# A decoder trunk on one core: a fourth weight block summed by an accumulating transfer, and table transfers moved ahead of the first MLP

## The chip, the cores and the metric

The kernel runs on 1 core of a Trainium2 chip. The metric is the device time of one execution in microseconds (us), as the median of several runs.

Engines are named as in the profile: PE (TensorE, matrix products), PEld (its weight loads), DVE (VectorE), ACT (ScalarE), POOL (GpSimd), SP (SyncE). SP and POOL each issue transfers (DMAs) in the order of their own queue. A transfer issued by POOL can add what it brings to what lies at its destination; this is called an accumulating transfer here.

## The reference, cut to what matters

A two-layer decoder trunk on 512 tokens of width 1024, all in float32. Layer 0 is attention and an MLP, layer 1 a gated short convolution and an MLP:

```python
def conv_ffn(h, norm_g, w_up, conv_w, w_down):
    xn = rms_norm(h, norm_g)
    u = causal_dwconv(xn @ w_up, conv_w)          # w_up: 1024 x 5632, conv over 3 tokens
    g, val = u[..., :D_FF], u[..., D_FF:]         # D_FF = 2816
    return (jax.nn.silu(g) * val) @ w_down

h = x
for layer in range(DEPTH):                        # DEPTH = 2
    i = layer // 2
    if layer % 2 == 0:
        h = h + attention_mixer(h, ...)
    else:
        h = h + short_conv_mixer(h, ...)
    h = h + conv_ffn(h, ffn_norm[layer], ffn_w_up[layer], ffn_conv[layer], ffn_w_down[layer])
```

## The kernel before

Float32 operands are split into a high and a low half (`whi` on ACT, `wlo` on DVE), and each product is three matmuls (high by high, high by low, low by high). The activations lie with features on the partitions and 512 tokens in the free dimension.

**The up-projection with seven products.** Most of the up-projection is not done as a plain product. The weight of one group (256 gate columns and the 256 value columns that belong to them) is cut in two halves of the depth (512 rows each) and two halves of the columns (gate, value), which gives four blocks of 512 x 256; the tokens are cut in two halves as well. A Strassen-like scheme (`Sevens`) then makes the result with seven products of half size, called p1, p7, p3, p6, p2, q5, q4. Their weights are sums of blocks with one, two, three or four members. In the code a block is `block_of(g, kh, half)`: `kh` the half of the depth, `half` 0 for gate and 1 for value.

- X is the block (0, 0), used for p1; afterwards POOL adds the block (0, 1) to it in place (L1105), and the sum serves q5.
- Y serves p7; it is a sum of two blocks.
- "three" serves p6, a sum of three blocks; "four" serves q4, the sum of all four.
- W is the block (1, 0), for p2; Z the block (1, 1), for p3.

X and Y have two buffers each. W, Z, three and four come into the ring `raw` (three buffers of 128 x 1056 numbers).

`Sevens.slot(g, s)` issues one product in slot s = 0 to 6 of group g (p3 of the group before stands in slot 2), and around it the loads, splits and evacuations that come due. The first MLP makes its groups 0 and 1 by plain products (`PLAIN`) and groups 2 to 10 in this way; the second MLP makes all eleven so. Small pieces of other work ("chores", with costs and a credit) are strewn between the slots.

**The tables.** The sums for Y, three and (in the first MLP only) four are not made on DVE. POOL makes them ahead of time in DRAM: `table_steps(layer)` is a generator of which each step issues one DRAM-to-DRAM transfer, in turn a plain copy (L117) and an accumulating one (L114). Table 7 is block (1, 1) plus block (0, 1); table 6 is a copy of table 7 plus (0, 0); table 4 is a copy of table 6 plus (1, 0). The groups are taken in three chunks (`CHUNKS`), the 512 rows in two parts. So the first MLP has 3 x 2 x 6 = 36 steps, the second 3 x 2 x 4 = 24. Each step but the first of a table part waits for the step before it, since it reads or adds to what that one wrote. `pin` keeps instructions in the order of the program on their queue.

Where the steps are issued:

- the 36 steps of the first MLP between the units of attention, two in each unit;
- 8 steps of the second MLP (`FAR`) after attention, ahead of the output projection's end;
- 9 (`BETWEEN`) at the end of `mlp(0, ...)`, after its last product; since POOL's queue runs ahead of PE, these start when POOL's last transfer for the down-projection is out;
- the last 7 in the convolution layer (`sum_far(99)`).

**In the second MLP** there is no table 4: once p6 has taken its halves from "three", an accumulating transfer adds the block (1, 0) to it in place (slot 2), and q4 takes its halves from the same buffer. In the last group DVE adds W to it instead. The lines of slot 2 that choose:

```python
if self.fours:
    self.load_one(g, "four", self.table("4", g))
else:
    c["four"] = c["three" if self.table else "Y"]
    if self.scaled and soon:
        self.add_block(g, "four", 1, 0)
    else:
        dve.tensor_tensor(c["four"], c["four"], c["W"], op=ALU.add)
```

`fours` is true for the first MLP, `scaled` for the second, `soon` as long as a group follows. The convolution layer uses `Sevens` with no tables.

**The down-projections** (L1673) use seven products too. Their weight blocks come by SP (L285, L291) and by accumulating transfers of POOL (L289) into buffers whose names end in "chain"; for q5 some are loaded as "other" and added on DVE (L286). Around the same time POOL adds halves of the activations (`head_blocks`, `hs_b_blocks`, L1070). Weights of plain products are loaded by SP at L309 into raw and split at L315 (ACT) and L316 (DVE).

Of the kernel before, what the change touches and what calls it, by code (L numbers as in the profile page):

```python
# [22 lines left out]
ALU = mybir.AluOpType  # L23
# [24 lines left out]
FILL1, FILL2, BEFORE = 1.5, 3.3, 2.0  # L48
UNITS = (0, 1), (2,), (3,)
PLAIN = 2, 0  # L50
FAR, BETWEEN = 8, 9
CHUNKS = ((2, 3), (5, 3), (8, 3)), ((0, 3), (3, 4), (7, 4))
EARLY, LATER = 4.0, 5.0
SHARE = 0.58
# [3 lines left out]
def trunk(  # L58
# [9 lines left out]
    class InOrder:  # L68
        def __init__(self, engine):
            self.engine = engine  # L70
# [6 lines left out]
    act, dve, pe, pool = InOrder(nc.scalar), InOrder(nc.vector), nc.tensor, nc.gpsimd  # L77
# [19 lines left out]
    tables = {}  # L97

    def table_steps(layer):

        w = ffn_w_up[layer]
        for n in "76" if layer else "764":
            for g, m in CHUNKS[layer]:
                tables[layer, n, g] = far.tile([512, m * 256 + 16], F32, tag=f"t{layer}{n}{g}", name=f"t{layer}{n}{g}")
        def block(kh, half, g, m):
            return w[kh * 512:(kh + 1) * 512, half * DFF + g * 256:half * DFF + (g + m) * 256]
        for g, m in CHUNKS[layer]:
            for rows in (slice(0, 256), slice(256, 512)):
                for step in range(4 if layer else 6):
                    n = "764"[step // 2]  # L110
                    to = tables[layer, n, g][rows, 0:m * 256]
                    if step % 2:
                        src = block(*((0, 1), (0, 0), (1, 0))[step // 2], g, m)
                        pin(nc.gpsimd.dma_start(to, src[rows, :], accum_op=ALU.add))  # L114
                    else:
                        src = block(1, 1, g, m) if step == 0 else tables[layer, "76"[step // 2 - 1], g][:, 0:m * 256]
                        pin(nc.gpsimd.dma_start(to, src[rows, :]))  # L117
                    yield

    def table_of(layer, n, group):  # L120
        g, m = next(c for c in CHUNKS[layer] if c[0] <= group < c[0] + c[1])
        return tables[layer, n, g][:, (group - g) * 256:(group - g + 1) * 256].rearrange("(k p) c -> p k c", p=P)
# [128 lines left out]
    def fill(us):  # L251
        quota[0] += us
        while quota[0] > 0 and fillers:
            before = clock[0]
            if next(fillers[0], None) is None:
                fillers.pop(0)
            quota[0] -= clock[0] - before

    def run(gen):
        for _ in gen:  # L260
            pass
# [582 lines left out]
    def output_begin():  # L844
        last_w.append([weights(), weights(AHEAD - 1)])
        yield from output_part(range(4), range(2), "b")
        last_w.append([weights(AHEAD - 1), weights(0)])
        yield from output_part(range(4), (2,), "b")
# [116 lines left out]
            fillers.append(values(g + 1))  # L965
    units = [(p, u) for p in range(8) for u in range(len(UNITS))]
    waiting = {}
    sums_far = table_steps(0)
    next(sums_far)
    fill(PRE)  # L970
    for g in range(len(units) + 2):
        for _ in range(2):
            next(sums_far, None)
        if g < len(units):
            waiting[g] = logits(*units[g])
            fill(FILL1)
        if g == len(units):
            fillers.append(output_begin())
            fill(BEFORE)
        if g >= 2 and units[g - 2][1] == len(UNITS) - 1:  # L980
            p = units[g - 2][0]
            weigh(p)
            if p == 3:
                fillers.append(output(0, residual))
        if 1 <= g <= len(units):
            for b, w in waiting.pop(g - 1):
                turn(units[g - 1][0], b, w)
                fill(FILL2 / len(UNITS[units[g - 1][1]]))
    fill(1e9)

    run(sums_far)
    sums_far = table_steps(1)

    def sum_far(n):
        for _ in range(n):
            next(sums_far, None)

    sum_far(FAR)

    def residual_out(o, acc, nxt):  # L1000
        dve.tensor_tensor(h[:, o, :], acc, h[:, o, :], op=ALU.add)
# [81 lines left out]
    class Sevens:  # L1083

        def __init__(self, name, mp, groups, block_of):
            self.name, self.mp, self.groups, self.block_of = name, mp, groups, block_of
            self.forms = {n: [mp.tile([P, 4, HT], F32R, tag=f"{n}_{i}", name=f"{n}_{i}{name}") for i in ("hi", "lo")] for n in FORMS}
            self.st, self.wides, self.table, self.fours, self.scaled = {}, {}, None, False, False

        def load_pair(self, g):  # L1090
            s = self.st[g] = {}
# [66 lines left out]
        def slot(self, g, s):  # L1158

            on, was, soon = (i in self.groups for i in (g, g - 1, g + 1))  # L1160
            if self.chores:
                self.work_off(self.rate(g, s))
            form, n, fresh = (("p1", "A", True), ("p7", "T", True), ("p3", "R", False), ("p6", "R", False), ("p2", "A", False),
                              ("q5", "R", False), ("q4", "T", False))[s]
            if s == 2:
                if was:
                    self.product(g - 1, form, n, fresh)
            elif on:
                self.product(g, form, n, fresh)
            st, p, c = self.st, g - 1, self.st.get(g)  # L1170
            if s == 0:
                if was:
                    if "p3" not in st[p]:
                        self.weights_of(p, "p3", "Z")
                    self.join(p, "yg", st[p]["T"], st[p]["Xs"])
                if on:
                    self.load_one(g, "W", self.block_of(g, 1, 0))
                if soon:
                    self.load_pair(g + 1)
            elif s == 1:  # L1180
                first = not was
                if on and first and not self.ahead and "p6" not in c:
                    self.weights_of(g, "p6", "three" if self.table else "Y")
                if on:
                    act.activation(self.bank_of(g, "R"), c["A"], AF.Copy, scale=-1.0)
                if on and not first:
                    self.weights_of(g, "p6", "three" if self.table else "Y")
                if soon and not self.table:
                    self.add_block(g + 1, "Y", 1, 1)
            elif s == 2:  # L1190
                if on:
                    self.kept(g, "P7s", c["T"])
                    if "p2" not in c:
                        self.weights_of(g, "p2", "W")
                    if self.fours:
                        self.load_one(g, "four", self.table("4", g))
                    else:
                        c["four"] = c["three" if self.table else "Y"]
                        if self.scaled and soon:
                            self.add_block(g, "four", 1, 0)  # L1200
                        else:
                            dve.tensor_tensor(c["four"], c["four"], c["W"], op=ALU.add)
            elif s == 3:
                if was:
                    self.early(p, st[p]["R"])
                if on:
                    self.weights_of(g, "q5", "X")
            elif s == 4:
                if on:
                    self.kept(g, "Xs", c["R"])  # L1210
                    self.weights_of(g, "q4", "four")
            if was and s != 2:
                self.tail(p, s)
            if s == 5:
                if on:
                    self.load_one(g, "Z", self.block_of(g, 1, 1))
                    self.open_wides(g)
                    self.left(g, c["A"])
                if soon:
                    self.weights_of(g + 1, "p1", "X")  # L1220
                elif on and self.ahead:
                    self.weights_of(g, "p3", "Z")
            elif s == 6:
                if on:
                    self.join(g, "yv", c["R"], c["P7s"])
                if soon:
                    self.first_sums(g + 1)
# [17 lines left out]
    def up_begin(layer, norm, mp, place):  # L1245
# [4 lines left out]
        w_up, base = ffn_w_up[layer], PLAIN[layer]  # L1250
# [5 lines left out]
        up = Sevens(layer, mp, range(base, HF), block_of)  # L1256
        up.norm, up.chores = norm, []
        up.table = lambda n, g: table_of(layer, n, g)
        up.fours, up.scaled = layer == 0, not base
        up.rate = lambda g, s: 1.4 if g == base else 0.3 if layer else 0.5  # L1260

        def wides_of(g):
# [249 lines left out]
    def mlp(layer, norm, mp, begun_up=None):  # L1512
# [21 lines left out]
        def block(kh, ch, k0, fresh):  # L1534
            return (ffn_w_down[layer], kh * HF + k0, ch * 512), fresh
# [165 lines left out]
                    finish(b)  # L1701
        if after_:
            after_.finish()
            sum_far(BETWEEN)
        return after_

    with tc.tile_pool(name="mlp0", bufs=1, reuse_waits="tile") as mp:
# [6 lines left out]
    with tc.tile_pool(name="mlp1", bufs=1, reuse_waits="tile") as mp:  # L1714
        norm = Norm("n3", 8)
        blocks, up = up_begin(1, norm, mp, rp)
# [77 lines left out]
```

## Time and profile before

| | us |
|---|---|
| runs | 1122.01, 1123.62, 1126.45 (median 1123.62) |
| profiled execution | 1121.57 |
| its span in the profile | 1119.8 |
| PE busy, DVE busy, ACT busy, POOL busy | 1109.3, 958.8, 680.4, 174.3 |

How to read it: the profile is one execution; times inside it count from the start of its span. PE is busy for nearly the whole span, but a matmul is counted as busy from its start to its modelled end, and matmuls overlap, so short holes do not show in the busy time; the number of matmuls in a stretch shows them. The stages by time: attention with its output projection and then the plain groups of the first MLP to 320, its seven-product groups to about 496, its down-projection to about 611, the convolution layer to about 783, the second MLP to the end. The granted PE clock is 1.00 throughout.

### The profile page before, as it was taken

To read this page: it belongs to the slowest core of one execution; us is meant where nothing else is said; L and a number is where in the kernel's file an instruction comes from. 1 tells how busy PE (TensorE), PEld (TensorE's weight loads), DVE (VectorE), ACT (ScalarE), POOL (GpSimd) and SP (SyncE) were. 2 spreads that over 40 slices of the span, in tenths; PEclk is the share of its full clock that TensorE was granted. 3 is DMA by queue.
4 is the path that set the end of the run, shared out by engine and by line. 5 is a ranking of instruction groups with operands and counts; after the bars stand their busy time and mean duration, and the time that the engine had idled before them with its cause. 6 is when DMAs were issued, how large, how long until landed. Compare 5 with 4: busy or idle time off the path is not lost.

```text
span 1119.8 us, 19731 instructions
## 1 busy us (share of the span) xinstructions
PE 1109.3 (99%) x7803; PEld 1011.9 (90%) x7803; DVE 958.8 (86%) x1482; ACT 680.4 (61%) x1006; POOL 174.3 (16%) x203
## 2 busy tenths in 40 slices
PE   9999999999999999999999999999999999999998
PEld 7888787878899999999999889988999999998886
DVE  6798988987899787888979899767899999999886
ACT  7466676655466667676547355445666656667553
POOL 4011111111111110014401101110112221014300
PEclk9999999999999999999999999999999999999999
DMA  6668777677888787699997955697879877899951
GB/s 195 178 175 199 177 186 196 164 197 196 245 206 199 189 212 192 195 297 198 224 260 195 238 143 141 130 275 178 207 179 218 204 189 189 217 262 205 230 154 57
DMA packets 180012, 220.90 MB, mean 197 GB/s; under 512 B 7788, under 2 KB 143516, under 8 KB 179920
## 3 DMA queue, kind: packets, MB, share of 16 engines
q0 software_dynamic: 48384, 97.43, 43.9%
q1 hardware_dynamic: 131376, 122.14, 34.7%
q8 instruction: 61, 1.00, 0.4%
q14 instruction: 31, 0.25, 0.1%
q10 hardware_dynamic: 160, 0.07, 0.0%
HBM read 214.64 MB, written 53.48 MB: 239 GB/s over the span
## 4 chain that ended last, share of the span: by engine, by line
PE 82%; DVE 7%; DMA 5%; issue 3%; ACT 2%; SPq 0%; ACTq 0%; DVEq 0%; POOLq 0%
PE psb L1078 28%; PE psa L1078 11%; PE psb L1673 10%; PE psa L1673 7%; PE psb L336 4%; PE psb L338 4%; PE psb L337 4%; PE psb L710 2%; PE psa L807 2%; DVE wlo L316 1%; DMA Xc<-in_conv_w_in 1%; DMA raw<-in_conv_w_in 1%; DMA raw<-in_conv_w_out 1%; PE psc L782 1%; PE psa L338 1%
## 5 line engine op out<-in xcount | busy, mean ns | idle before, releaser
L1078 PE MATMUL psb<-p_lo,whi_p 128*128 128x256 f32 x480 | 135.1, 282 | 0.0
L315 ACT ACTIVATE whi<-raw 128x1024 fp32r<-128x1024 f32 (+2 forms) x81 | 83.3, 1029 | 85.3 <-PE psb L337 27.9
L1078 PE MATMUL psb<-p_hi,wlo_p 128*128 128x256 f32 x480 | 135.0, 282 | 0.0
L1078 PE MATMUL psb<-p_hi,whi_p 128*128 128x256 f32 x480 | 134.8, 281 | 0.0
L316 DVE TENSOR_TENSOR wlo<-raw,whi 128x1024 fp32r<-128x1024 f32 (+2 forms) x81 | 95.8, 1183 | 28.0 <-ACT whi L315 27.6
L1078 PEld LDWEIGHTS psb<-p_hi,whi_p 128*128 128x128 f32 x480 | 90.9, 189 | 0.0
L1078 PE MATMUL psb<-q_hi,whi_q 128*128 128x256 f32 x320 | 89.9, 281 | 0.5 <-ACT whi_q L74 0.5
L1078 PEld LDWEIGHTS psb<-p_lo,whi_p 128*128 128x128 f32 x480 | 90.4, 188 | 0.0
L1078 PEld LDWEIGHTS psb<-p_hi,wlo_p 128*128 128x128 f32 x480 | 90.2, 188 | 0.1
L1078 PE MATMUL psa<-p_hi,wlo_p 128*128 128x256 f32 x320 | 90.1, 282 | 0.0
L1078 PE MATMUL psa<-p_lo,whi_p 128*128 128x256 f32 x320 | 90.1, 281 | 0.0
L1078 PE MATMUL psb<-q_lo,whi_q 128*128 128x256 f32 x320 | 90.0, 281 | 0.0
L1078 PE MATMUL psb<-q_hi,wlo_q 128*128 128x256 f32 x320 | 89.9, 281 | 0.0
L1078 PE MATMUL psa<-p_hi,whi_p 128*128 128x256 f32 x320 | 89.8, 281 | 0.0
L336 PE MATMUL psb<-hs_a,whi 128*128 128x512 f32 x192 | 79.3, 413 | 0.0
L338 PE MATMUL psb<-hs_a,wlo 128*128 128x512 f32 x192 | 76.3, 398 | 0.0
L1673 PE MATMUL psb<-act,whi 128*128 128x256 f32 x352 | 63.1, 282 | 0.5 <-DVE act L1031 0.4
L1078 PEld LDWEIGHTS psb<-q_hi,whi_q 128*128 128x128 f32 x320 | 60.6, 189 | 0.8 <-ACT whi_q L74 0.8
L1078 PEld LDWEIGHTS psa<-p_hi,whi_p 128*128 128x128 f32 x320 | 60.6, 190 | 0.1
L1078 PEld LDWEIGHTS psa<-p_lo,whi_p 128*128 128x128 f32 x320 | 60.2, 188 | 0.1
L1078 PEld LDWEIGHTS psb<-q_lo,whi_q 128*128 128x128 f32 x320 | 60.2, 188 | 0.0
L1078 PEld LDWEIGHTS psa<-p_hi,wlo_p 128*128 128x128 f32 x320 | 60.2, 188 | 0.0
(553 smaller groups left out, 3593.6 us busy)
## 6 DMA issues: line engine op xcount, KB each, us to landing
t<-in_ffn_w_up POOLq DMA_DIRECT2D x30, 768.0 KB, 7.8
raw<-in_attn_w_in SPq DMA_DIRECT2D x24, 512.0 KB, 5.4
t<-in_ffn_w_up POOLq DMA_DIRECT2D x12, 1024.0 KB, 10.9
t<-t POOLq DMA_DIRECT2D x14, 768.0 KB, 4.7
X<-in_ffn_w_up SPq DMA_DIRECT2D x20, 512.0 KB, 5.0
Y<-t SPq DMA_DIRECT2D x20, 512.0 KB, 6.7
three<-t SPq DMA_DIRECT2D x20, 512.0 KB, 4.8
W<-in_ffn_w_up SPq DMA_DIRECT2D x20, 512.0 KB, 4.0
```

The source lines that it names most:

```text
L315: return (act.activation(hi[:, at_], raw[:, at_], AF.Copy), dve.tensor_tensor(lo[:, at_], raw[:, at_], f32(hi[:, at_]), op=ALU.subtract))
L316: dve.tensor_tensor(lo[:, at_], raw[:, at_], f32(hi[:, at_]), op=ALU.subtract))
L336: made = [pe.matmul(acc, w[0], rhs[0], start=first, stop=False), pe.matmul(acc, w[0], rhs[1], start=False, stop=False), pe.matmul(acc, w[1 ...
L337: pe.matmul(acc, w[0], rhs[1], start=False, stop=False),
L338: pe.matmul(acc, w[1], rhs[0], start=False, stop=last)]
L710: pe.matmul(ss[e][:, c:c + wide], ql[rows, b * P:n], kl[rows, 0:wide], start=first and b == bs[0], stop=last and b == bs[-1])
L782: pe.transpose(t[:, k * P:(k + 1) * P], w[:, e, k * P:(k + 1) * P], ident)
L807: pe.matmul(out_, w, t[:, first:first + step * (NB - k - 1) + 1:step, :], start=k == 0 and i == 0, stop=k == NB - 1 and i == 1)
L1078: pe.matmul(to, w[a][:, k, c], x[b][:, k, :], start=fresh and i + k + t == 0, stop=i == 1 and k == 3 and t == 2, skip_group_check=not fresh)
L1673: pe.matmul(to, l, r, start=begin and o + t == 0, stop=end and t == 2 and o == (0 if layer else 1), skip_group_check=not fresh)
```

## The change

The first MLP has no table 4 any more: `table_steps` makes tables 7 and 6 for both layers, so the first MLP has 24 steps instead of 36. In slot 2 the branch `fours` is gone, and the accumulating transfer into "three" is used wherever there are tables and a group follows, in the first MLP too: in its groups 2 to 9 POOL adds the block (1, 0) to "three" where SP loaded "four", and in group 10 DVE adds W to it.

The steps of both layers become one generator, issued from the units of attention: one step ahead, and then two in each unit until `FAR` = 41 are out, that is the 24 of the first MLP and 17 of the second. The 8 steps after attention and the 9 at the end of the first MLP are gone from there; the last 7 stay in the convolution layer.

```diff
-FAR, BETWEEN = 8, 9
+FAR = 41
...
-        for n in "76" if layer else "764":
+        for n in "76":
...
-                for step in range(4 if layer else 6):
-                    n = "764"[step // 2]
+                for step in range(4):
+                    n = "76"[step // 2]
...
-    sums_far = table_steps(0)
-    next(sums_far)
+
+    def both_layers():
+        for layer in range(2):
+            yield from table_steps(layer)
+
+    sums_far = both_layers()
+
+    def sum_far(n):
+        for _ in range(n):
+            next(sums_far, None)
+
+    sum_far(1)
     fill(PRE)
     for g in range(len(units) + 2):
-        for _ in range(2):
-            next(sums_far, None)
+        sum_far(max(0, min(2, FAR - 1 - 2 * g)))
...
-    run(sums_far)
-    sums_far = table_steps(1)
-
-    def sum_far(n):
-        for _ in range(n):
-            next(sums_far, None)
-
-    sum_far(FAR)
...
-                    if self.fours:
-                        self.load_one(g, "four", self.table("4", g))
+                    c["four"] = c["three" if self.table else "Y"]
+                    if self.table and soon:
+                        self.add_block(g, "four", 1, 0)
                     else:
-                        c["four"] = c["three" if self.table else "Y"]
-                        if self.scaled and soon:
-                            self.add_block(g, "four", 1, 0)
-                        else:
-                            dve.tensor_tensor(c["four"], c["four"], c["W"], op=ALU.add)
+                        dve.tensor_tensor(c["four"], c["four"], c["W"], op=ALU.add)
...
-        up.fours, up.scaled = layer == 0, not base
+        up.scaled = not base
...
             after_.finish()
-            sum_far(BETWEEN)
```

More of the change, by code (lines that the diff above doesn't have):

```diff
@@ L108, in table_steps @@
             for rows in (slice(0, 256), slice(256, 512)):
-                for step in range(4 if layer else 6):
-                    n = "764"[step // 2]
+                for step in range(4):
+                    n = "76"[step // 2]
                     to = tables[layer, n, g][rows, 0:m * 256]
                     if step % 2:
-                        src = block(*((0, 1), (0, 0), (1, 0))[step // 2], g, m)
+                        src = block(*((0, 1), (0, 0))[step // 2], g, m)
                         pin(nc.gpsimd.dma_start(to, src[rows, :], accum_op=ALU.add))
                     else:
-                        src = block(1, 1, g, m) if step == 0 else tables[layer, "76"[step // 2 - 1], g][:, 0:m * 256]
+                        src = block(1, 1, g, m) if step == 0 else tables[layer, "7", g][:, 0:m * 256]
                         pin(nc.gpsimd.dma_start(to, src[rows, :]))
@@ L1087, in __init__ @@
             self.forms = {n: [mp.tile([P, 4, HT], F32R, tag=f"{n}_{i}", name=f"{n}_{i}{name}") for i in ("hi", "lo")] for n in FORMS}
-            self.st, self.wides, self.table, self.fours, self.scaled = {}, {}, None, False, False
+            self.st, self.wides, self.table, self.scaled = {}, {}, None, False
         def load_pair(self, g):
```

## The prediction

> **What bounds the kernel now.** I read the page first (busy time, then the chain that ended last), then the stretches by time with their counts of matmuls, then the instructions of POOL in order, and last the DVE, ACT and landing rows around the places where TensorE (PE) was late.
>
> ```profile
> span 1119.8 us, 19731 instructions
> PE 1109.3 (99%) x7803; PEld 1011.9 (90%) x7803; DVE 958.8 (86%) x1482; ACT 680.4 (61%) x1006; POOL 174.3 (16%) x203
> PE 82%; DVE 7%; DMA 5%; issue 3%; ACT 2%; SPq 0%; ACTq 0%; DVEq 0%; POOLq 0%
> ```
>
> PE is the bound. Its busy share hides short gaps, though, so I count matmuls. The columns below are the stretch, its length, and busy time with count for PE, PEld, DVE, ACT, POOL, then granted clock, DMA share and GB/s.
>
> ```profile
> 340.00:480.00 140.00, 140.00 (x1186) 140.00 (x1185) 115.92 (x144) 93.54 (x121) 15.25 (x13) 1.00 0.73 194
> 520.00:560.00 40.00, 40.00 (x340) 40.00 (x340) 36.73 (x53) 23.51 (x32) 17.05 (x17) 1.00 1.03 213
> 560.00:600.00 40.00, 38.56 (x321) 37.95 (x320) 32.43 (x43) 21.07 (x31) 2.92 (x4) 1.00 0.94 255
> 600.00:610.00 10.00, 9.95 (x84) 9.75 (x83) 8.85 (x13) 7.82 (x12) 0.88 (x1) 1.00 0.61 145
> 660.00:670.00 10.00, 9.39 (x77) 8.99 (x76) 9.10 (x8) 6.91 (x9) 2.58 (x2) 1.00 0.88 174
> 820.00:1000.00 180.00, 180.00 (x1524) 180.00 (x1523) 169.91 (x217) 114.24 (x140) 31.83 (x26) 1.00 0.85 208
> 1060.00:1100.00 40.00, 40.00 (x174) 32.08 (x173) 33.50 (x43) 23.38 (x32) 2.42 (x2) 1.00 0.52 131
> ```
>
> The up-projections of both MLPs (340 to 480, 820 to 1000) run at 118 ns for each 128x256 matmul (140/1186, 180/1524), without a hole. So nothing that is taken from DMA or DVE there can shorten them; a change can only open a hole. Holes are at 560 to 610, in the down-projection of the first MLP: 321 matmuls where the 40 us before hold 340, and 84 where 85 fit. 20 missing matmuls of 0.118 us make 2.4 us. At 660 to 670 (start of the convolution layer) 8 are missing, 0.9 us. The same down-projection stage of the second MLP (1060 to 1100, 128x512 matmuls of 230 ns) has no hole.
>
> What is late at 560 to 600 is weights. In the chain that ended last, and in the landing times of the stretch 555 to 612 (first three issue rows) against 1060 to 1116 in the second MLP (last two):
>
> ```profile
> 564.02 8.58 DMA raw<-in_ffn_w_down
> 622.97 13.81 DMA raw<-in_conv_w_in
> ...
> t<-in_ffn_w_up POOLq DMA_DIRECT2D x5, 1024.0 KB, 10.7
> raw<-in_ffn_w_down SPq DMA_DIRECT2D x2, 512.0 KB, 8.6
> other<-in_ffn_w_down SPq DMA_DIRECT2D x2, 512.0 KB, 5.4
> ...
> raw<-in_ffn_w_down SPq DMA_DIRECT2D x2, 512.0 KB, 5.2
> other<-in_ffn_w_down SPq DMA_DIRECT2D x2, 512.0 KB, 3.4
> ```
>
> The same loads land in 8.6 and 5.4 us in the first MLP and in 5.2 and 3.4 us in the second. The first has the table transfers of the second MLP beside them (t, 1024 KB each), and these are what the change moves away. POOL's rows in order of time (start, duration):
>
> ```profile
> 40.20 0.59 POOL L117 DMA_DIRECT2D t<-in_ffn_w_up  x1
> 258.98 0.88 POOL L117 DMA_DIRECT2D t<-in_ffn_w_up  x1
> 283.41 0.91 POOL L117 DMA_DIRECT2D t<-in_ffn_w_up  x1
> 304.33 0.89 POOL L114 DMA_DIRECT2D t<-in_ffn_w_up  x1 [3.99 <-DMA t<-t]
> 319.48 1.34 POOL L1105 DMA_DIRECT2D X<-in_ffn_w_up  x1 [14.26 <-DVE wlo_p L1029]
> 557.68 1.09 POOL L117 DMA_DIRECT2D t<-in_ffn_w_up  x1
> 620.87 0.88 POOL L117 DMA_DIRECT2D t<-in_ffn_w_up  x1
> ```
>
> The nine steps written behind the first MLP start at 557.68, as soon as POOL's last sum for the down-projection is issued, and go on to 620.87.
>
> **The change part by part.**
>
> *Nine table steps leave 557 to 621.* Gain between 0 (the loads are late for another reason) and 2.4 us (all 20 matmuls). I take 2.4: the second MLP, with the same loads and no table beside them, is whole. Behind it the 13.81 us load of convolution weights, which ran beside the last tables, held ACT 1.78 us and through it DVE 1.25 us:
>
> ```profile
> 636.88 1.06 ACT L315 ACTIVATE whi<-raw 128x1024 fp32r<-128x1024 f32 x1 [1.78 <-DMA raw<-in_conv_w_in]
> 637.98 1.23 DVE L316 TENSOR_TENSOR wlo<-raw,whi 128x1024 fp32r<-128x1024 f32 x1 [1.25 <-ACT whi L315]
> ```
>
> DVE then works without pause until the hole at 660 to 670. Between 0 and 0.9 us comes back; I take 0.6, since DVE's backlog there is mostly its own work (9.10 of 10 us). Late next is that DVE backlog.
>
> *The table steps before the first MLP.* They are a chain on POOL, each waiting for the transfer before it, so their time is transfer time. Now 36 steps of the first MLP run from 40.20 to 258.98 (six units of six, 36.5 us each); a unit of four with 768 KB steps takes 283.41 - 258.98 = 24.4 us. After: six units of 24.4 for the first MLP, two more for the second, then two with 1024 KB (4/3 of it, 32.6): 40.2 + 195 + 65 = 300.5, where the 17th step of the second MLP is issued, to land some 10.7 later, at 311. Now the last one before the first MLP is issued at 304.33. The stream is as long as before and carries the same bytes (32 of 768 KB and 9 of 1024 against 44 of 768). POOL has nothing else until X at 319.48. I cost this at nothing. The cover is that no engine but POOL waits for table transfers in attention; if it failed, the 17th step would have to slip 19 us before X is issued late. The seven steps left stay in the convolution layer.
>
> *Eight accumulating transfers in the first MLP.* For each of the groups 2 to 9, SP's load of four (512 KB) and its place in the ring raw go; POOL issues a transfer that adds a fourth block into three, once both halves of p6 have been taken from it. That is a new wait, on wlo_p<-three; behind it on POOL stands only the next block sum or X, over 10 us later. The second MLP does exactly this now. Rows for one group of the first MLP, its first group, and landing times (min/median/max) of three in 820 to 1000 and of X in 335 to 480:
>
> ```profile
> 401.61 1.22 DVE L1029 TENSOR_TENSOR wlo_p<-three,whi_p 128x1024 fp32r<-128x1024 f32 x1
> 408.72 1.05 ACT L1027 ACTIVATE whi_q<-four 128x1024 fp32r<-128x1024 f32 x1
> 410.07 1.22 DVE L1029 TENSOR_TENSOR wlo_q<-four,whi_q 128x1024 fp32r<-128x1024 f32 x1
> 411.01 5.70 PE psb L1078 x48
> ...
> 321.56 1.23 DVE L1029 TENSOR_TENSOR wlo_p<-three,whi_p 128x1024 fp32r<-128x1024 f32 x1
> 329.26 1.05 ACT L1027 ACTIVATE whi_q<-four 128x1024 fp32r<-128x1024 f32 x1
> 331.51 5.67 PE psb L1078 x48
> ...
> L1105 POOL DMA_DIRECT2D three<-in_ffn_w_up x8: 1283/1283/1296, 830.7 to 968.7; - x8
> DMA to landing us min/median/max: 5.1/5.7/6.4
> ...
> DMA to landing us min/median/max: 4.8/6.3/8.9
> ...
> PE psb L1078 <- ACT whi_q L74: 0.5, 1, 0.5
> ```
>
> The add can go at 402.83, say 403.0; at 5.7 us it lands at 408.7, when ACT takes four today. The 48 matmuls from 411.01 are q5 and q4, so q4 begins at 413.86 and wants wlo_q at 414.1 (its third product). Today wlo_q ends at 411.29, 2.8 us before that, so the add may land as late as 411.5: 8.5 us after its issue. With the second MLP's 5.1 to 6.4 nothing stalls; with the slowest X (8.9) 0.4 us in a group. I take 0 for the seven steady groups, nearest to the row of the same transfer. In the first group the add goes at 323.0 and lands between 328.7 (5.7 us) and 331.9 (8.9 us). ACT takes four at 329.26 today, so it would be held for up to 2.6 us; q4 begins at 331.51 + 2.84 = 334.35 and is still served, but the split for the next group moves close to its use. The second MLP's first group lost 0.5 us of PE to this very transfer (last row, from PE's waits in 780 to 1000). Cost between 0 and 1.5 (a landing of 10.8, below); I take 0.5.
>
> Issue took 1.28 us and landing at most 6.4 in the second MLP, beside a DVE busy 169.91 of 180 us. [...]
>
> *Group 10 adds on DVE* (no next group), where four was a load. In the second MLP:
>
> ```profile
> L1202 DVE TENSOR_TENSOR three<-three,W x1: 1215/1215/1215, 988.9 to 988.9; 128x1024 f32<-128x1024 f32 x1
> ```
>
> 1.2 us on DVE, covered by its idle time (115.92 of 140 us busy in 340 to 480), 1.2 on the path if that is gone; the second MLP shows no hole after it. I take 0. SP loses nine issues; it is not on the chain.
>
> Sum: -2.4 - 0.6 + 0.5 = -2.5 us. Against the profiled execution (1121.57 us, span 1119.8) that is 1119.1; the median of the runs shown, 1123.62, lies 2.05 above it, so 1121.1, rounded 1121.0.
>
> **The rivals.**
>
> *Order, not traffic.* The loads at 560 to 600 are late because SP issues them late (buffers), and stay late without the tables. For it: waits of SP for DVE's splits are its longest. Against: the landing itself, from issue, is 8.6 against 5.2. Gain 0, cost 0.5: 1124.1.
>
> *Adds that land late (the other side).* Place: ACT's split of four at q4, in groups 2 to 9. It opens a hole once a landing exceeds 8.5 us, and decides from 9.6 on ((5.6 + 3.3) / 8 = 1.1 us in each group). Accumulating transfers in a crowded stretch do take that long:
>
> ```profile
> X_chain<-in_ffn_w_down POOLq DMA_DIRECT2D x4, 512.0 KB, 10.8
> ```
>
> At 10.8: 2.3 x 8 = 18.4 us, less 3.3 of gain: 1138.7. Against: the stretch in question moves 194 GB/s, less than the second MLP's 208, where 6.4 was the worst. I leave it 0.08, since the first MLP orders its ACT work otherwise. [...]
>
> *More than the holes counted.* All 3.3 us come back, the first group costs nothing, and attention gains some 2.4 us from tables that load it differently: 1117.9. Against: in 40 to 320 PE waits for no transfer.
>
> *A table stream that ends too late.* 7% longer units put the 17th step at 319.5 and X behind it. X lands at 327 now and its next use by PE (q5) is at 331.51, so a slip of 26 us (10%) costs about 4 us: 1123.62 - 3.3 + 4 = 1124.3.
>
> **How the numbers follow.** Forecast 0.60 (1121.0), order 0.18, late adds 0.08, more 0.10, late stream 0.04. A measurement of this kernel tells about 0.5%, 5.6 us, from no change (its runs spread 1122.01 to 1126.45). Below 1118.0 lies only "more": faster 0.10. Above 1129.2 late adds, and 0.02 of a worse late stream: slower 0.10. The rest, same 0.80. The range goes from all gains with a run at the low end of the spread (1123.62 - 4.7 - 1.6 = 1117.3, so 1117) to no gain with 1.5 us of cost and 0.9 of spread (1126). The likeliest case alone spans 1119 to 1123.
>
> **What the changed profile would show.** Right: no t row on POOL between 311 and 700; raw<-in_ffn_w_down landing in about 5 us and 340 matmuls in the 40 us that answer to 560 to 600; about 85 in the 10 us at the start of the convolution groups; three<-in_ffn_w_up 18 times instead of 10, landing below 8.5 us, no four<-t, and 8.47 matmuls a microsecond kept through the first up-projection; the last early t on POOL near 300. Wrong: PE waiting for whi_q or wlo_q in the first MLP, t rows still running beside X at 319, or holes at 560 to 600 that stay with no table beside them.

## The result and the profile after

| | before | after |
|---|---|---|
| median of 14 runs each, us | 1122.65 (1120.97 to 1126.45) | 1120.09 (1119.51 to 1122.06) |
| ratio, 95% interval | | 0.9978 (0.9969 to 0.9987) |
| profiled execution and its span, us | 1121.57, 1119.8 | 1119.51, 1117.7 |

The kernel became 2.6 us faster by the medians and 2.1 us by the profiled executions, about 0.2%: a small gain, but the interval leaves out 1. From the page of after: the span, the busy times, and the shares of the chain that ended last.

```profile
span 1117.7 us, 19713 instructions
PE 1110.0 (99%) x7803; PEld 1013.5 (91%) x7803; DVE 960.4 (86%) x1483; ACT 681.6 (61%) x1006; POOL 174.7 (16%) x199
PE 91%; DVE 4%; DMA 2%; ACT 1%; issue 1%; SPq 1%; DVEq 0%; ACTq 0%
```

PE's busy time hardly differs (1109.3 before, 1110.0 now); what differs is the chain: 5% of the span hung on DMA before, 2% now. The same stretches by time as in the prediction follow (stretch, length, busy time and count of PE, PEld, DVE, ACT, POOL, clock, DMA share, GB/s). The start of the convolution groups lies 2 us earlier now, so it is read at 658 to 668.

```profile
340.00:480.00 140.00, 140.00 (x1186) 140.00 (x1185) 115.55 (x143) 94.02 (x121) 24.41 (x20) 1.00 0.81 193
560.00:600.00 40.00, 39.97 (x338) 39.77 (x337) 34.40 (x46) 22.64 (x33) 1.30 (x1) 1.00 0.59 157
598.00:608.00 10.00, 9.92 (x84) 9.71 (x84) 8.85 (x13) 7.55 (x11) 0.00 (x0) 1.00 0.03 5
658.00:668.00 10.00, 10.00 (x85) 9.84 (x84) 8.43 (x8) 6.59 (x10) 2.29 (x2) 1.00 0.94 196
820.00:1000.00 180.00, 180.00 (x1518) 180.00 (x1517) 169.39 (x215) 113.38 (x139) 31.22 (x26) 1.00 0.85 205
```

321 matmuls at 560 to 600 have become 338 (340 would fill it), and the 10 us at the start of the convolution layer hold 85 instead of 77. The first up-projection still holds 1186 in 140 us: the eight accumulating transfers opened no hole. The issues of 555 to 612, with the median time to the landing (from the issue until the data are there):

```profile
raw<-in_conv_w_in SPq DMA_DIRECT2D x4, 512.0 KB, 3.8
raw<-in_ffn_w_down SPq DMA_DIRECT2D x2, 512.0 KB, 6.8
other<-in_ffn_w_down SPq DMA_DIRECT2D x2, 512.0 KB, 3.8
```

The down-projection's weights land in 6.8 and 3.8 us, where they took 8.6 and 5.4. These medians stand on few loads: `raw` x2 has only one landing on record in either run, and not that of the same load. Load by load, the second of `raw` took 8.2 us in the first experiment below, with the table steps beside it, and 6.8 in after; the third took 8.6 in before and 4.7 in the second experiment, without them. Of the two of `other`, one went from 7.7 to 4.4, and the other stayed (3.2 and 3.3). POOL's rows in order of time (start, duration), and the rows of the tile `three` in 320 to 480 (durations in ns, first and last start, landing times, who waited):

```profile
40.42 0.59 POOL L117 DMA_DIRECT2D t<-in_ffn_w_up  x1
280.86 0.90 POOL L117 DMA_DIRECT2D t<-in_ffn_w_up  x1
319.70 1.36 POOL L1105 DMA_DIRECT2D X<-in_ffn_w_up  x1 [37.94 <-DVE wlo_p L1029]
323.31 1.29 POOL L1105 DMA_DIRECT2D three<-in_ffn_w_up  x1 [2.24 <-DMA Z<-in_ffn_w_up]
...
L1105 POOL DMA_DIRECT2D three<-in_ffn_w_up x8: 1273/1288/1303, 323.3 to 463.4; - x8
...
DMA to landing us min/median/max: 3.7/5.9/7.2
```

The last early table step leaves at 280.86, 39 us ahead of X, and the longest landing is 7.2 us, where the prediction gave 8.5 as the slack.

To place the gain, the i-th matmul of before was set against the i-th of after (after minus before, by their starts in the two profiled executions): +0.23 us up to 570, -1.73 at 600, -2.67 at 670, -3.03 at 720, then -2.1 at the end. So 2.0 us come from the down-projection, 0.9 from the start of the convolution layer and 0.4 from small holes up to 720. Of the 0.9 us given back, 0.2 lie between 783 and 820, where PE waits 0.2 us for a value of DVE at 785, and 0.7 in the second up-projection, where this execution's matmuls came a little slower (1518 in 180 us against 1524), on which more below.

### The profile page after: what moved, and what is told of

Same layout as the page of the kernel before. It is cut to its first block, busy times and chain, and to the rows that moved or that the text cites. A ratio compares the mean times of both kernels' runs of the same rounds, so it can differ in the third digit from the quotient of the medians.

```text
span 1117.7 us, 19713 instructions
## 1 busy us (share of the span) xinstructions
PE 1110.0 (99%) x7803; PEld 1013.5 (91%) x7803; DVE 960.4 (86%) x1483; ACT 681.6 (61%) x1006; POOL 174.7 (16%) x199
## 4 chain that ended last, share of the span: by engine, by line
PE 91%; DVE 4%; DMA 2%; ACT 1%; issue 1%; SPq 1%; DVEq 0%; ACTq 0%
PE psb L1078 30%; PE psa L1078 12%; PE psb L1670 11%; PE psa L1670 8%; PE psb L336 5%; PE psb L338 5%; PE psb L337 5%; PE psb L710 2%; PE psa L807 2%; PE psa L338 1%; DMA raw<-in_conv_w_out 1%; PE psa L337 1%; PE psa L336 1%; PE psc L782 1%; PE psb L592 1%
```

## The experiments

Two theories were set against each other. **Traffic**: the nine table transfers, running beside the last weight loads of the first down-projection, made those loads late; moving them is the gain. **Adds**: the gain comes from table 4 and the loads of `four` being dropped (10 MB of 221 MB less to move), and the place of the steps matters little. In each session the kernel before ran beside the edited ones on the same chip (its medians were 1123.5 to 1124.7, against the 1122.65 above), and a ratio is always to these runs; times of different sessions compare less well.

**Nine steps put back behind the first MLP**, all else as after:

```diff
-FAR = 41
+FAR, BETWEEN = 32, 9
...
             after_.finish()
+            sum_far(BETWEEN)
```

> The changed kernel with nine of its seventeen early steps of the second MLP's tables put back at the end of the first MLP (32 steps in attention, 9 behind the down-projection); the accumulating transfers and the missing table 4 stay. Traffic theory (the nine transfers beside the last weight loads make the holes): the holes at 560 to 610 and 660 to 670 come back, some 2.0 and 0.9 us, and the time is that of the kernel before, 1122.6 us (ratio 1.000). Adds theory (fewer bytes and no loads of four make the gain): no holes, 1120.1 (ratio 0.998).

Measured: 1122.04 us, ratio to before 0.9993 (0.9972 to 1.0014). Its stretches, and its issues in 555 to 612:

```profile
560.00:600.00 40.00, 38.10 (x317) 37.50 (x317) 31.96 (x42) 20.98 (x31) 2.92 (x4) 1.00 0.92 246
658.00:668.00 10.00, 9.68 (x79) 9.27 (x78) 9.26 (x10) 5.64 (x8) 2.58 (x2) 1.00 0.72 134
```

```profile
t<-in_ffn_w_up POOLq DMA_DIRECT2D x5, 1024.0 KB, 10.9
raw<-in_conv_w_in SPq DMA_DIRECT2D x3, 512.0 KB, 5.8
raw<-in_ffn_w_down SPq DMA_DIRECT2D x2, 512.0 KB, 8.2
other<-in_ffn_w_down SPq DMA_DIRECT2D x2, 512.0 KB, 5.6
```

Both holes are back, with landings as late as before, although table 4 stays dropped. By the matmul's index this execution loses 0.5 us on before between 560 and 600, where after gains 2.0, and gains 0.3 at the start of the convolution layer, where after gains 0.9; the profiled execution (1122.23) is no shorter than before's (1121.57). The times alone don't decide: the interval of the ratio holds both forecasts, 1.000 and 0.998. The traces do, and Traffic holds for both holes. It is not shown for the 0.4 us up to 720: the small hole there closes in this run too (0.7 us between 700 and 720), with the steps back.

**The move alone**: the kernel before, with table 4 and the loads of `four` kept; the nine steps are strewn over the slots of the first MLP's groups:

```diff
-FAR, BETWEEN = 8, 9
+FAR = 8
...
+            if layer == 0 and i % 7 == 3:
+                sum_far(1)
...
-            sum_far(BETWEEN)
```

> The kernel before, with table 4 and SP's loads of four kept, and only the nine steps moved: one in slot 3 of each of the groups 2 to 10 of the first MLP, where POOL is idle for most of 20 us. Traffic theory: holes at 560 to 610 and 660 to 670 go, 1120.0 us (ratio 0.998), as with the whole change. Adds theory: nothing gained, 1122.6 (ratio 1.000).

Measured: 1120.75 us, ratio 0.9968 (0.9952 to 0.9983).

```profile
340.00:480.00 140.00, 140.00 (x1186) 140.00 (x1185) 116.00 (x143) 94.21 (x122) 20.87 (x20) 1.00 0.93 247
560.00:600.00 40.00, 39.97 (x338) 39.77 (x338) 34.52 (x47) 22.65 (x33) 1.28 (x1) 1.00 0.61 160
658.00:668.00 10.00, 10.00 (x85) 9.84 (x85) 9.13 (x9) 6.61 (x9) 2.60 (x2) 1.00 0.84 156
```

The holes are gone without a single byte dropped: Adds falls as the source of the gain. The up-projection carries 247 GB/s (193 in after) and keeps its 1186 matmuls, so that stage had room for the nine steps. One hole of about a microsecond appeared at 508 (PE waited 0.7 us for `wlo` of a weight); its cause is open.

**Five of the nine back** (`FAR, BETWEEN = 36, 5`, else as the first experiment):

> As e1_nine_back, but only five steps behind the down-projection (36 in attention). They run from 557 to about 604. Traffic theory, hole by hole: the holes at 560 to 600 come back in full (2.0 us), the one at 660 to 670 stays away, since no table is beside the convolution's first weights; 1122.1 us less what the second hole is worth, so about 1121.9. If the hole at 660 to 670 came from DVE's own backlog and not from the late load, it comes back too: 1122.6.

Measured: 1122.83 us, ratio 0.9985 (0.9970 to 1.0000).

```profile
560.00:600.00 40.00, 39.05 (x328) 38.64 (x327) 33.13 (x45) 22.31 (x32) 4.28 (x5) 1.00 0.95 255
658.00:668.00 10.00, 10.00 (x85) 9.84 (x84) 9.24 (x9) 6.25 (x8) 2.60 (x2) 1.00 0.69 111
```

The five steps run from 559 to about 600. The hole beside them is back in part (328 matmuls, between 317 and 338; 1.2 us late by the matmul's index, less than the 2.0 expected), and the one at 660, which they no longer reach, stays closed. PE's waits in 560 to 605, first with nine steps back, then with five:

```profile
572.30 0.39 PE L1670 MATMUL psa<-act,whi 128*128 128x256 f32 x1 [0.82 <-DVE act L1031]
576.07 0.39 PE L1670 MATMUL psa<-act,whi 128*128 128x256 f32 x1 [0.68 <-DVE act L1031]
592.36 0.39 PE L1670 MATMUL psb<-act,whi 128*128 128x256 f32 x1 [0.40 <-DVE act L1031]
...
573.65 0.39 PE L1670 MATMUL psa<-act,whi 128*128 128x256 f32 x1 [0.92 <-DVE act L1031]
```

Only the first of the three waits is left, although the same five steps run beside this stretch in both. DVE splits the third load of `raw` at the same time (574.19 and 574.20), but PE comes 1.3 us later here, mostly since its matmuls ran slower before (1181 in 340 to 480 against 1186), so it has less to wait for. So where the steps are decides whether there is a hole, but not alone how deep it is. The hole at 660 has a second possible cause that no run separates: with nine steps ahead of it, POOL's own sum into `Yc` for the convolution layer is issued at 621.44 in before instead of 592.98 in after and 596.10 here, and is then in flight beside the 13.81 us load as well. The times of the first and this run overlap: for the split between the holes only the traces speak.

**No accumulating transfer in the first MLP**: DVE adds W instead, table 4 stays dropped.

```diff
-                    if self.table and soon:
+                    if self.scaled and soon:
```

> The changed kernel with the fourth block added by DVE in groups 2 to 9 of the first MLP as well (1.2 us each), so no accumulating transfer into three there. If the transfer costs nothing where it is and DVE has 1.2 us to spare in each group of 20 (it is busy 83% there): same time, 1120.1 within 0.5 us, and no hole from 340 to 480. If DVE's order is the limit: up to 8 x 1.2 = 9.6 us more, 1129.7.

Measured: 1121.22 us, ratio 0.9969 (0.9954 to 0.9985). DVE is 9 us busier in 340 to 480 and PE has no hole there:

```profile
340.00:480.00 140.00, 140.00 (x1181) 140.00 (x1181) 124.58 (x152) 93.58 (x122) 15.37 (x13) 1.00 0.65 168
```

The ratio is that of the second experiment (0.9968), so the accumulating transfer itself carries nothing of the gain that can be seen, and the sum could be made on DVE. The time is 1.1 us above the 1120.1 that was expected within 0.5: by the matmul's index the profiled execution gains the holes (1.3 of the 2.0 us between 570 and 600, 0.9 at the start of the convolution layer), and loses 1.0 to a slower pace of matmuls up to 570 and 1.3 between 900 and 960, where PE waits 0.7 us for `wlo_q` of DVE. That wait stands in some runs and not in others (0.5 us with the nine steps back, none in before and after); why is open.

**All seventeen steps before the first MLP, with table 4 kept** (the kernel before with `FAR = 17` and no steps behind the first MLP):

> The kernel before with table 4 kept, and all seventeen steps of the second MLP behind the 36 of the first, ahead of the first MLP: what moving alone gives if table 4 stays. By the length of the stream (36.5 us for a unit of six, 24.4 and 32.6 for the units of the second MLP) the seventeenth step is issued at 259 + 49 + 65 = 373 instead of 300, so the transfer into X of group 2, due at 319.5, is issued some 54 us late on POOL, and q5 of the first group waits for it. PE's slack there is about 4 us: about 50 us more, 1172. If POOL's order did not matter, 1120.

Measured: 1171.55 us (two runs, 1168.07 and 1175.03), ratio 1.0419 (1.0375 to 1.0463). POOL's rows, PE's waits in 300 to 420 (total, times, longest), and the stretches:

```profile
365.70 0.87 POOL L117 DMA_DIRECT2D t<-in_ffn_w_up  x1
366.26 1.70 POOL L1105 DMA_DIRECT2D X<-in_ffn_w_up  x1
```

```profile
PE psb L1078 <- ACT Xs L1139: 49.6, 1, 49.6
```

```profile
340.00:360.00 20.00, 0.00 (x0) 0.00 (x0) 0.00 (x0) 0.00 (x0) 1.39 (x2) 0.50 0.71 154
380.00:400.00 20.00, 18.89 (x147) 18.89 (x148) 19.50 (x26) 16.03 (x23) 1.28 (x1) 0.89 0.65 169
400.00:420.00 20.00, 20.00 (x171) 20.00 (x170) 16.13 (x20) 13.29 (x18) 3.73 (x3) 1.00 0.88 222
```

X stands behind the table steps in POOL's queue and leaves at 366.26 instead of 319.48; PE stands still for 49.6 us. That the 50 us came out is in part luck: X leaves 46.8 us late, not 54, but then takes 12.6 us to land instead of 6.2, so it lands 53.1 us late, and PE's slack was 3.5. This is what the other half of the change is for: with table 4 dropped, the first MLP's stream is 12 steps shorter, and the seventeen fit ahead of X. It is not the only way: the move into the up-projection's slots got the same gain with table 4 kept.

**The add made twice** in groups 2 to 9 of the first MLP, to measure the slack of the accumulating transfer:

```diff
                     if self.table and soon:
                         self.add_block(g, "four", 1, 0)
+                        if not self.scaled:
+                            self.add_block(g, "four", 1, 0)
```

> The changed kernel with the accumulating transfer into three issued twice in groups 2 to 9 of the first MLP, the second waiting for the first (the fourth block is counted twice in the sum, which leaves the output's value aside). It doubles the landing from about 6 to about 12 us. By the slack of the prediction (a landing of 8.5 us after the issue still serves q4) this opens a hole of 12 - 8.5 = 3.5 us in each of eight groups: about 28 us more, 1148. If the slack is really larger, by ACT and DVE catching up, less: a slack of 12 us gives 1120.

Measured: 1171.38 us, ratio 1.0418 (1.0380 to 1.0455), far above what was expected. PE's waits in 300 to 540, then three stretches of 20 us, and the first of them in after:

```profile
PE psb L1078 <- ACT whi_q L1027: 26.6, 8, 5.3
PE psb L1078 <- DVE wlo_q L1029: 4.6, 8, 0.8
```

```profile
380.00:400.00 20.00, 14.24 (x106) 13.74 (x105) 11.61 (x17) 7.25 (x10) 4.36 (x4) 0.83 0.64 148
440.00:460.00 20.00, 17.46 (x122) 17.25 (x123) 13.38 (x17) 12.68 (x17) 3.47 (x3) 0.83 0.76 169
480.00:500.00 20.00, 15.47 (x111) 14.97 (x110) 10.36 (x12) 7.86 (x11) 3.85 (x3) 0.84 0.58 120
```

```profile
380.00:400.00 20.00, 20.00 (x172) 20.00 (x171) 16.30 (x21) 13.43 (x18) 3.82 (x3) 1.00 0.89 206
```

The waits are 31.2 us, 3.9 in each of eight groups. From the first issue to the second landing it takes 12.1 to 14.9 us, 13.0 in the mean, more than the 12 expected. Less PE's waits, group by group, that leaves a slack of 8.8 to 9.2 us (9.7 in the first group), where the prediction read 8.5: nearly right. The other 20 us (1171.4 - 1120.1 = 51.3, less 31.2) are in the clock column. Finer stretches show how:

```profile
336.40:343.20 6.80, 5.74 (x25) 5.45 (x26) 6.16 (x8) 3.50 (x6) 1.28 (x1) 0.50 0.62 181
343.30:363.70 20.40, 17.65 (x147) 17.24 (x145) 14.45 (x19) 12.04 (x17) 2.55 (x2) 1.00 0.73 147
363.70:367.10 3.40, 3.00 (x14) 3.00 (x15) 3.40 (x5) 1.46 (x2) 2.16 (x2) 0.51 0.54 142
```

At each of the eight holes the clock is halved for 6.8 us (six times) or 3.4 us (twice), 47.6 us in all, and then full again. In the first of these rows a matmul takes 0.23 us of PE's busy time (25 in 5.74 us), in the second 0.12 us (147 in 17.65). By that, as an estimate, half the clock over 47.6 us costs up to 23.8 us, so the 20 fit.

**The last seven steps moved too** (after, and the slot line of the second experiment, so that none is left in the convolution layer), and then also DVE adding W in the second MLP's first group, where PE waits 0.6 us for `whi_q`:

```diff
+            if layer == 0 and i % 7 == 3:
+                sum_far(1)
...
-                    if self.table and soon:
+                    if self.table and soon and (was or not self.scaled):
```

> The changed kernel with the last seven table steps taken from the convolution layer as well and issued one in slot 3 of each of the groups 2 to 8 of the first MLP. By the traffic theory the load of the convolution's output weights that takes 12.1 us beside them gets shorter, and the small holes at 700 to 720 (0.4 us) and 785 (0.35 us) go: 1119.4 us, 0.7 less than the changed kernel. If these holes have other causes, 1120.1. The eight accumulating transfers in the first MLP stay in time (a table step is issued after the add, and the next POOL instruction follows some 10 us later).

> As e6_last_seven, and in the first group of the second MLP DVE adds W to three (1.2 us) where an accumulating transfer of 5.8 us held ACT and PE for 0.8 us. If that transfer is what PE waits for there, 0.8 us less than e6_last_seven: 1118.6. If DVE, which is full at that place, becomes the wait, no gain or up to 1.2 us more.

Measured: 1119.66 us, ratio 0.9953 (0.9936 to 0.9970), with the steps alone; 1121.81, ratio 0.9977 (0.9963 to 0.9990), with the DVE add. The second is a miss, 2.1 us more where at most 1.2 were expected. PE's waits in 780 to 1000, with the steps alone, then with the add:

```profile
PE psb L1078 <- ACT whi_q L74: 0.8, 1, 0.8
```

```profile
PE psb L1078 <- DVE wlo_q L1029: 0.4, 1, 0.4
PE psb L1078 <- ACT whi_q L74: 0.2, 1, 0.2
```

In the first group the wait shrank from 0.8 to 0.2 us, but by the matmul's index nothing was gained between 783 and 820 (0.3 us lost against before, 0.2 with the steps alone). The 0.4 us for `wlo_q` lie elsewhere, at 938, in a later group, and are the wait that came with the sum on DVE in the first MLP as well. DVE is 93% busy in that up-projection. The two profiled executions are equally long (spans of 1118.0 us), so what makes the medians differ by 2.1 us is open. Since the version with the steps alone looked better than after, both were run once more side by side on one chip:

> The kernel after, unchanged, beside the version with the last seven steps moved too, on one chip. Traffic theory: median 2.5 us below the kernel before (ratio 0.9978 as measured), holes at 560 to 600 and 658 to 668 gone.

> The last seven table steps in the first MLP's groups, as in the run before of this kind. Traffic theory: the small holes between 690 and 785 go, 0.5 to 0.8 us, so 0.5 to 0.8 us below the kernel after on the same chip. Rival (nothing is late there, since PE covers it): equal to the kernel after within 0.3 us. A difference of 2.5 us, as the two sessions apart would give, is expected by neither.

Measured: 1119.82 (after, ratio 0.9963, 0.9944 to 0.9982) and 1120.15 (last seven moved, ratio 0.9954, 0.9927 to 0.9981). They can't be told apart; the apparent lead came from comparing different sessions. In 700 to 720 the traces count 169 matmuls in this run of after and 171 with the seven moved, about 0.2 us. The transfers themselves did become faster: in 680 to 790 the eight loads of the convolution's output weights land in 3.7 us (median) with no table beside them, in 9.5 with the seven steps there (8.0 in the first run of after). So a load that lands sooner brought no time that can be seen where PE hardly waits for it.

## Why the prediction was right, point by point

- **Nine steps leave 557 to 621, -2.4.** Measured -2.0 by the matmul's index. Of 20 missing matmuls 3 are still missing (338 of 340, and 84 of 85 in the 10 us behind), 0.35 us. Shown by two experiments: steps back, holes back; steps moved alone, holes gone. The prediction's row of landings, 8.6 against 5.2 us, was not of like loads: 8.6 is the third load alone, 5.2 the median of the second and third (6.0 and 4.4). Like for like it read the same way: 8.6 against 4.4. The second load still takes 6.8 in after, so the tables were not all that slowed it, but enough for PE.
- **Convolution layer, between 0 and 0.9, taken 0.6.** Measured 0.9, the upper end. The choice rested on DVE's backlog being its own work; DVE was 9.10 of 10 us busy there, and in stretches that start at the same matmul it is 8.18 in after (from 658.25), in the second experiment (659.25) and in the third (660.42). So more of the backlog came from the late weights than was allowed. (The rows of 658 to 668 above show 9.13 and 9.24 for these two experiments because their matmuls come later.)
- **Table stream at no cost.** Right, with more room than said: the last step leaves at 280.86, not at 300.5. Half of the difference is the unit of 24.4 us, which was read from a single unit at the end of the stream: the eight units took 20.2 to 25.1, 23.2 in the mean. The other half is the two units with 1024 KB, put at 32.6 by their bytes: they took 27.5.
- **Steady groups, 0.** Right: no PE wait in 310 to 560, landings up to 7.2 against 8.5.
- **First group, +0.5.** This term was mis-sized: it cost 0. `whi_q` is split from `three` at 329.66 where it was split from `four` at 329.26, and q4 begins only some 4.7 us later (334.35 in the prediction), so the difference was taken up. (POOL's next transfer, `head_blocks`, follows 2.2 us behind the add in this group, not over 10; no PE wait came of it.) The 0.5 of the second MLP's first group didn't carry over.
- **Group 10's DVE add, 0.** Right; no hole shows.
- **Issue and landing beside a busy DVE.** Right: in the first MLP the transfers into `three` were issued in 1.27 to 1.30 us and landed in 3.7 to 7.2, with DVE 115.55 of 140 us busy. The second MLP's, which the prediction took as the model, had 1.28 to 1.30 and 5.1 to 6.4, with DVE 169.91 of 180.
- **The rivals.** "Order, not traffic" is refuted by the first two experiments. "Late adds" didn't come, but its point of decision was real: doubling the transfer brought holes, at a slack of about 9 us. "A late table stream" was a matter of 39 us of room, not of 19 (and X landed at 325.7 in before, not at 327). "More" would have needed gains in attention; by the matmul's index there are none (+0.23 up to 570).
- **The sum.** -2.5 forecast; -2.1 between the profiled executions, -2.6 between the medians of 14. The mechanism was right; that the sum comes so near is in part luck. The first term was 0.4 too large, the second 0.3 too small, the 0.5 of the first group did not come, and 0.4 gained up to 720 and 0.9 lost behind it were not in the sum at all; these errors, of both signs, left 0.4 between them. The forecast time lies 0.9 us above the measured one mainly since the median of the three runs shown, 1123.62, stood 1.0 above the median of 14.

## What to carry to other kernels

Count matmuls in a stretch, beside another stretch with the same work, to find the holes that a busy share of 99% hides, and look at what shares the transfers with the loads that end last there. Work that has no deadline, such as a table for a later stage, is worth moving out of a stretch where loads are late into one where they are not, even a busy one (in the second experiment the up-projection, which kept its 1186 matmuls at 247 GB/s instead of 194); how long it may be in another engine's queue ahead of something urgent decides where it can go (17 steps with table 4 kept cost 49.6 us of waiting, without it nothing). A load that got faster is worth nothing where nothing waits for it (3.7 us instead of 9.5 for the output weights here, and no time that can be seen). And a slack is measured by doubling the thing that uses it and taking the waits off the longer time (8.8 to 9.2 us here, where the reading of the trace gave 8.5).

## What was not expected of the hardware

**With the add made twice, the holes cost more than their length.** With waits of 2.3 to 5.3 us in each of eight groups of some 26 us, the granted PE clock fell to 0.83 over 20 us stretches, and 31.2 us of holes cost 51.3. At each of the eight holes the clock was halved for 3.4 or 6.8 us, also in the five groups whose longest wait was 2.3 to 3.0 us (a second one of 0.5 to 0.8 followed about 1.3 us later). In the single hole of 49.6 us the clock row reads 0.50 while PE stands still, 0.89 in the 20 us where it starts again, and 1.00 from there. The holes that this change closes, 2.4 us in sum and 0.9, were not followed by a lower clock in the profiled execution of before: the longest single wait among them is 0.7 us, and the clock rows at 560 to 610 and at 660 to 670 read 1.00, as they do in after (at 560 to 608 and 658 to 668).

In other executions the clock is not always full. Of the 81 of the kernel before that ran beside the experiments, 27 had a mean granted clock of 0.998 or less, and took 1123.9 to 1135.4 us; of after's 26 executions 2 did. Among those with 1.000 the medians are 1122.6 (37 of before) and 1119.7 (16 of after). Whether the holes of before bring this on is not shown: 4 of the 12 executions with the sum on DVE had 0.998 too, with most of the holes gone.

**The pace of matmuls differed a little between executions.** The second run of the unchanged kernel after shows, in the stretch that held 1186 matmuls in the first:

```profile
340.00:480.00 140.00, 140.00 (x1181) 140.00 (x1180) 116.00 (x143) 94.04 (x120) 24.41 (x20) 1.00 0.82 194
```

That is 118.5 ns for each instead of 118.0, without a hole, 0.6 us in this stretch alone. Slower stretches of this kind occurred in runs of several edits too (1181 with the sum on DVE and with five steps back), and up to 570 it cost the profiled execution with the sum on DVE 1.0 us, more than a third of what was measured. What sets it stays open.
